# Hybrid decoder layer on one core: sample cross-attention on unsplit cache tiles, two couples fewer begun ahead, and a reordered feed-forward

## The chip, the core and the metric

The kernel runs on one core of a Trainium2 chip. The core has five engines, each with its own in-order instruction stream: TensorE (PE: matrix products into PSUM), VectorE (DVE), ScalarE (ACT), GpSimd (POOL) and SyncE (SP). Nearly all transfers between the chip's memory (HBM) and the core's SBUF are issued from SP, one after another, and carried out by 16 DMA engines. The metric is the device time of one launch in microseconds (us), the median of several runs.

## The reference, cut to what matters

One decoder layer, in fp32, for a prompt of 1024 tokens and eight sample sequences of 8 tokens each, width 1024. The branches ahead of the cross-attention are not touched by the change.

```
x <- LN1(alpha*x + branches(x))
qm = (x @ w_mq)                                  # 4 heads x 256
s  = einsum('nqhe,nkhe->nhqk', qm, mem_k) / 16   # 256 memory tokens
pr = softmax(s)
att = einsum('nhqk,nkhe->nqhe', pr, mem_v) @ w_mo
x <- LN2(alpha*x + att)
ff = square(relu(x @ w_up)) @ w_down             # 1024 -> 4096 -> 1024
x <- LN3(alpha*x + ff)
```

For the prompt, mem_k and mem_v are computed once. For the eight sample sequences they come from a cache with keys and values of each sequence's own: 8 x 256 x 1024 numbers each, 16.8 MB in all.

## The kernel before

Most products are made in the form float32r, in which a value is split into a high half (`whi`, `ah`, a rounding copy made by ACT) and a low half (`wlo`, `al`, the rest, a subtraction on DVE). One product of two split operands is three matmuls: high by high, high by low, low by high. A plain fp32 product of unsplit operands is also possible; the profile counts it as two matmul records (two passes).

**Cross-attention of the samples** (`sample_x`). This generator runs beside the prompt's cross-attention: each `yield` hands over to the prompt's scores (`sc`, line 129). The cache comes in 32 tiles of 128x1024 numbers (512 KB). `split_w` loads a tile into `wraw`, ACT casts it to `whi` (line 100) and DVE makes `wlo` (line 106). Then come 8 matmuls for each tile with the sample's query `qz` (scores, `sps`, line 1553) or probabilities `pz` (outputs, `ops`, line 1578) as the stationary operand of 64 columns: high and low halves side by side, 32 columns each. After the outputs, `spread` turns them with products with a selection matrix `sel` (`otr`, line 1566).

**Feed-forward, up** (`feed`). The 4096 hidden columns are made in 16 couples p of two tiles of `w_up` rows (`fetch(p)`, 1 MB). For each couple a fast scheme (Strassen's, in Winograd's form) makes a 2x2 block product in 7 products instead of 8. The operands are sums of weight blocks (`sw`: two sums on POOL in `first_sums`, two on DVE in `prep`) and sums of blocks of the turned activations (`hat`, by names: "11", "21", "t1" to "t4", "22"), all split in halves (`split`: ACT line 1686, DVE line 1687; `xht`, `xlt` are the activations' halves). Each product is 24 matmuls of 272 columns, 12 for each of two column blocks c. Two of the seven ("11" and "21") need only activations that are ready early. `begin(p)` makes these two ahead for the couples p < `EARLY_PAIRS`, while the last parts of the activations are still being normed; the results of couples from 2 on are put into HBM (`vd`) from a buffer `vs` and fetched again by `recall`. The main loop then runs over p. In it `store(p-1)` issues the eight stores of the couple before, `fetch(p+2)` the loads of the couple after next, `sums_in` and `sums_out` move the sums of `w_down`.

All these transfers go through `dma`, which keeps them in the written order on SP. So a load stands behind each store that is written ahead of it, and a store waits until its sums (`sh` on POOL, lines 1925 to 1928) are made.

**Feed-forward, down** (`down`). Again 7 products, each over 16 couples: 112 steps (i, p), in the order of products 1, 2, 6, 7, 5, 3, 4. A step is 12 matmuls of 512 columns (`dn`, line 1989), for products 1, 2, 7 and 3 also two for the samples (line 1994). Before step n, `bring(n + LOADS)` issues loads and `cut(n + SPLITS)` splits the operands `dop` of the step that comes two steps later. The last product keeps its last `TAIL` couples back and does them token tile by token tile at the end, so that the last norms (`finish`) can start one tile after another.

A scheduler with instruction costs decides how the streams that the generators offer are interleaved; within an engine the order then is fixed.

Of the kernel before, what the change touches and what calls it, by code (L numbers as in the profile page):

```python
# [8 lines left out]
F32 = mybir.dt.float32  # L9
# [32 lines left out]
LOADS, SPLITS, TAIL, OX = 4, 2, 6, 12  # L42

EARLY_PAIRS = 6
# [5 lines left out]
class Kern:  # L50
# [1457 lines left out]
    def sample_x(self, x1, out):  # L1508

        nc, I, pm = self.nc, self.I, self.pm
        sel = pm.tile([64, 32], F32, name="sel")
        nc.sync.dma_start(sel, I["sel"])
        z = pm.tile([128, 512], F32, name="zs")
        qs = pm.tile([128, 8, 64], F32, name="qs")
        row = lambda name: pm.tile([128, 512], F32, name=name, tag="row", bufs=2)

        def own(src, name):

            t = pm.tile([128, 4, 4, 64], F32R, name=name, tag="own", bufs=2)
            nc.vector.memset(t.rearrange("p a s x -> p (a s x)").bitcast(F32), 0.0)
            t4 = t.rearrange("p (a b) s x -> p a b s x", b=2)
            for s4 in range(4):
                v, c = src(s4), 8 * s4
                nc.scalar.copy(t4[:, :, :, s4, c:c + 8], v)
                nc.vector.tensor_sub(t4[:, :, :, s4, 32 + c:40 + c], v, t4[:, :, :, s4, c:c + 8].bitcast(F32))
# [16 lines left out]
        parts = [(s2, hp) for s2 in range(2) for hp in range(2)]  # L1544
        for s2, hp in parts:
            qz = own(lambda s4: qs[:, 4 * hp:4 * hp + 4, 32 * s2 + 8 * s4:32 * s2 + 8 * s4 + 8].rearrange("p (a b) q -> p a b q", b=2), "qz")
            ps = self.wk_ps("sps", "acc")
            for s4 in range(4):
                w = self.split_w(I["cmk"][4 * s2 + s4, hp])
                for h in range(2):  # L1550
                    for ct in range(2):
                        for i in range(2):
                            nc.tensor.matmul(ps[0:64, h * 256:h * 256 + 256], qz[:, 2 * h + ct, s4, :], w[i][:, (2 * h + ct) * 256:(2 * h + ct) * 256 + 256],
                                             start=s4 == h == ct == i == 0, stop=s4 == 3 and h == ct == i == 1)
                yield
            r, lo = slice(64 * s2 + 32 * hp, 64 * s2 + 32 * hp + 32), row("slo")
            nc.scalar.copy(lo[r], ps[32:64])
            nc.vector.tensor_add(z[r], lo[r], ps[0:32])
        pT = pm.tile([128, 4, 128], F32, name="pTs")
        nc.scalar.copy(pT, self.keys_first(self.softmax(z, "ps")))  # L1560
        pT = pT.rearrange("p (h k) (s a t) -> p k h s a t", k=2, s=2, a=2)
        def spread(s2, hp, o):

            tr = self.wk_ps("otr")[:, 0:128].rearrange("p (k t) -> p k t", t=32)
            for k in range(4):
                nc.tensor.matmul(tr[:, k, :], o[0:64, k * 128:k * 128 + 128], sel, start=True, stop=True)
            nc.scalar.copy(out[:, 4 * hp:4 * hp + 4, 32 * s2:32 * s2 + 32], tr)

        last = None
        for s2, hp in parts:  # L1570
            pz = own(lambda s4: pT[:, :, :, s2, hp, 8 * s4:8 * s4 + 8], "pz")
            ps = self.wk_ps("ops", "acc")
            for s4 in range(4):
                w = self.split_w(I["cmv"][4 * s2 + s4, hp])
                for kb in range(2):
                    for h in range(2):
                        for i in range(2):
                            nc.tensor.matmul(ps[0:64, h * 256:h * 256 + 256], pz[:, 2 * kb + h, s4, :], w[i][:, (2 * kb + h) * 256:(2 * kb + h) * 256 + 256],
                                             start=s4 == kb == h == i == 0, stop=s4 == 3 and kb == h == i == 1)
                if s4 == 1 and last:  # L1580
                    spread(*last)
                yield
            o = row("so")
            nc.scalar.copy(o[0:64], ps[0:64])
            last = s2, hp, o
        yield
        spread(*last)
# [76 lines left out]
    def feed(self, hat, y, s_xb, s_y, w3, w4, wb):  # L1664
# [103 lines left out]
        hat.rest("t4")  # L1768
        s_y.close()
# [29 lines left out]
        def operands():  # L1799
            for p in range(16):  # L1800
# [5 lines left out]
        todo, ops = operands(), []  # L1806
# [40 lines left out]
        steps = [(i, p) for i in (1, 2, 6, 7, 5, 3, 4) for p in range(16)]  # L1847
# [18 lines left out]
        first_sums(0)  # L1866
        for p in range(16):
# [38 lines left out]
            if p < 14:  # L1906
                fetch(p + 2)
            else:
                for n in range(2):
                    bring(2 * (p - 14) + n)  # L1910
# [40 lines left out]
        self.down(ring4, steps, bring, cut, ready, slots, late, dma)  # L1951

    def down(self, ring4, steps, bring, cut, ops, slots, late, dma):
# [9 lines left out]
        v, u2, u3 = ([yp.tile([128, 512], F32, name=f"{x}{j}") for j in range(4)] for x in ("v", "u2", "u3"))  # L1963
# [20 lines left out]
        def tokens(n, j, first, last):  # L1984
            hs, w = ops[n]
            c = slice(j * 128, j * 128 + 128)
            parts = [(0, 0), (1, 0), (0, 1)]
            for k, (a, b) in enumerate(parts):
                nc.tensor.matmul(ps[j], hs[:, a, c], w[:, b], start=first and k == 0, stop=last and k == 2, skip_group_check=n >= 16 and steps[n][0] in (2, 7, 3))  # L1989
# [7 lines left out]
        def evict(i, j):  # L1997
# [3 lines left out]
            if i == 1:  # L2001
                nc.scalar.copy(v[j], ps[j])
            elif i == 2:
                keep(a[:, lo], ps[j])
            elif i == 6:
                nc.vector.tensor_add(u2[j], v[j], ps[j])
                keep(a[:, hi], u2[j])
            elif i == 7:
                nc.vector.tensor_add(u3[j], v[j], ps[j])
                for c in HALVES:  # L2010
                    keep(b[:, c], u3[j])
            elif i == 5:
                add(b[:, hi])
            elif i == 3:
                add(a[:, hi])
            else:
                nc.vector.tensor_sub(b[:, lo], b[:, lo], ps[j])

        def evict_sample(i):
# [3 lines left out]
            if i == 2:  # L2023
                nc.vector.scalar_tensor_tensor(lo, lo, ALPHA, sp[0:64], op0=ALU.mult, op1=ALU.add)
                nc.gpsimd.tensor_add(lo, lo, ex)
            elif i == 7:
                nc.vector.scalar_tensor_tensor(hi, hi, ALPHA, sp[0:64], op0=ALU.mult, op1=ALU.subtract)
                nc.gpsimd.tensor_sub(hi, hi, ex)
            elif i == 3:
                nc.vector.tensor_add(hi, hi, sp[0:64])  # L2030
                nc.gpsimd.tensor_add(hi, hi, ex)
# [11 lines left out]
        nsteps = len(steps)  # L2043
        for n, (i, p) in enumerate(steps):
            if n >= SPLITS:
                bring(n + LOADS)
            cut(n + SPLITS)
# [9 lines left out]
            if p == 0 and i in (1, 6, 5, 4):  # L2057
# [3 lines left out]
            starts = i in (1, 6, 5, 4)  # L2061
# [24 lines left out]
            if i == 3 and p < 4:  # L2086
# [100 lines left out]
def _consts():  # L2187
# [31 lines left out]
    return {"sel": np.tile(np.eye(32, dtype=f), (2, 1)), "cmask": cm, "amask": am, "tmask": tm, "smask": np.tile(sm, (128, 1)), "teye": te.reshape(128, 8, 32), "ident": np.eye(128, dtype=f)}  # L2219
# [98 lines left out]
```

## Time and profile before

| what | value |
|---|---|
| median of 3 runs | 2275.94 us (2272.01 to 2283.53) |
| the profiled execution's own time | 2281.47 us |
| its span, first to last instruction | 2279.7 us |
| mean granted TensorE clock | 0.977 of full speed |
| PE busy | 2175.1 us, 95% of the span, 13702 instructions |
| DVE, ACT, POOL busy | 1374.5 (60%), 978.7 (43%), 425.7 (19%) us |
| HBM traffic | 157 GB/s mean over the span |

In the profiled execution the branches end near 1297 us; then come the cross-attention (to 1443), the projection with `w_mo` and the second norm (to 1546), the first part of the feed-forward with its `begin` calls (to 1602), the up loop (to 1924), the down product (to 2268), and the last norm and stores. PE is the busiest engine in every one of these stages but the last, so the rows are read for two things: how long PE takes for its work, and where it waits.

### The profile page before, as it was taken

How to read it: one execution, taken by the hardware profiler on the slowest of the kernel's cores; microseconds unless marked ns; L12 is line 12 of the kernel's file. 1: busy time of each engine (PE TensorE's matmuls, PEld its weight loads, DVE VectorE, ACT ScalarE, POOL GpSimd, SP SyncE). 2: the span in 40 equal slices, each digit the busy share in tenths (PEclk: the TensorE clock that was granted, in tenths of full speed). 3: DMA queues.
4: the chain of work that ended last, by engine and by line, in shares of the span. 5: the costliest groups of instructions: out<-in, count | busy, mean ns of one | idle time of the engine just before them, and what ended most of it. 6: DMA issues, size and time to landing. Idle time of an engine off the chain costs nothing.

```text
span 2279.7 us, 36377 instructions
## 1 busy us (share of the span) xinstructions
PE 2175.1 (95%) x13702; PEld 1949.2 (86%) x13702; DVE 1374.5 (60%) x2748; ACT 978.7 (43%) x1888; POOL 425.7 (19%) x484
## 2 busy tenths in 40 slices
PE   8998999999999999999999999998789999999997
PEld 8987777898989888998998888778789999788886
DVE  3356767755665764343333877586667776655558
ACT  4333433145555655444231566335334444543432
POOL 0111111012311200123220500000445444100100
PEclk9998989999999999999999999999899999999999
DMA  5322333135444435555324355624487767975534
GB/s 191 103 75 61 99 90 98 38 129 186 152 132 130 130 114 171 162 173 162 102 64 149 120 190 167 221 102 141 162 292 261 248 238 239 325 240 182 178 118 171
DMA packets 186071, 359.41 MB, mean 158 GB/s; under 512 B 36312, under 2 KB 92776, under 8 KB 185896
## 3 DMA queue, kind: packets, MB, share of 16 engines
q1 hardware_dynamic: 175448, 321.52, 43.2%
q0 software_dynamic: 10448, 35.57, 4.6%
q8 instruction: 108, 1.77, 0.3%
q14 instruction: 67, 0.55, 0.1%
HBM read 252.18 MB, written 104.84 MB: 157 GB/s over the span
## 4 chain that ended last, share of the span: by engine, by line
PE 71%; DVE 10%; DMA 9%; issue 4%; ACT 3%; POOL 2%; SPq 1%; DVEq 0%; ACTq 0%; POOLq 0%
PE mm L117 21%; PE m L117 12%; PE dn L1989 11%; PE mm L129 8%; PE sc L129 3%; PE pp L117 3%; PE ds L1994 1%; DVE tpr L1013 1%; DVE wlo L106 1%; DMA vp<-in_vpages,pt 1%; ACT whi L100 1%; DMA Li<-Ld 1%; PE wtp L502 1%; DVE Ti L1014 1%; PE gr L965 1%
## 5 line engine op out<-in xcount | busy, mean ns | idle before, releaser
L117 PE MATMUL mm<-ah,whi 128*128 128x384 f32 (+1 forms) x1176 | 395.7, 336 | 8.4 <-ACT ah L277 4.9
L117 PE MATMUL mm<-al,whi 128*128 128x384 f32 (+1 forms) x1176 | 392.5, 334 | 0.6 <-DVE al L278 0.6
L117 PE MATMUL mm<-ah,wlo 128*128 128x384 f32 (+1 forms) x1176 | 391.7, 333 | 0.6 <-DVE wlo L106 0.6
L1989 PE MATMUL dn<-dop 128*128 128x512 f32 x1344 | 318.8, 391 | 3.7 <-ACT dop L1686 3.5
L1989 PEld LDWEIGHTS dn<-dop 128*128 128x128 f32 x1344 | 251.7, 188 | 60.6 <-ACT dop L1686 5.2
L106 DVE TENSOR_TENSOR wlo<-wraw,whi 128x1024 fp32r<-128x1024 f32 (+2 forms) x177 | 196.1, 1117 | 174.1 <-ACT whi L100 172.6
L100 ACT CAST whi<-wraw 128x1024 fp32r<-128x1024 f32 (+1 forms) x162 | 165.8, 1032 | 258.0 <-PE mm L117 101.6
L117 PEld LDWEIGHTS mm<-ah,whi 128*128 128x128 f32 x1176 | 224.4, 191 | 18.0 <-ACT ah L277 5.5
L117 PEld LDWEIGHTS mm<-al,whi 128*128 128x128 f32 x1176 | 224.1, 191 | 7.0 <-issue 3.5
L117 PEld LDWEIGHTS mm<-ah,wlo 128*128 128x128 f32 x1176 | 224.1, 191 | 4.3 <-issue 1.9
L1687 DVE TENSOR_TENSOR dop<-wraw,dop 128x512 fp32r<-128x512 f32 x224 | 151.3, 712 | 118.2 <-ACT dop L1686 117.6
L117 PE MATMUL m<-xht,wo 128*128 128x272 f32 x1024 | 202.7, 293 | 16.8 <-ACT wo L1686 10.5
L1686 ACT CAST dop<-wraw 128x512 fp32r<-128x512 f32 x224 | 131.2, 619 | 167.8 <-PE dn L1989 117.3
L117 PEld LDWEIGHTS m<-xht,wo 128*128 128x128 f32 x1024 | 165.8, 192 | 17.7 <-ACT wo L1686 10.7
L129 PE MATMUL mm<-wlo,ah 128*128 128x512 f32 (+1 forms) x488 | 170.1, 351 | 2.7 <-DVE wlo L106 2.7
L129 PE MATMUL mm<-whi,ah 128*128 128x512 f32 (+1 forms) x488 | 170.5, 351 | 0.8 <-ACT stA L300 0.5
L117 PE MATMUL m<-xh,wo 128*128 128x272 f32 x768 | 153.6, 293 | 6.1 <-DVE r L1901 6.1
L129 PE MATMUL mm<-whi,al 128*128 128x512 f32 (+1 forms) x448 | 156.5, 349 | 0.0
L117 PE MATMUL m<-xlt,wo 128*128 128x272 f32 x512 | 149.5, 292 | 0.0
L117 PEld LDWEIGHTS m<-xh,wo 128*128 128x128 f32 x768 | 124.7, 192 | 6.7 <-ACT wo L1686 2.6
L117 PE MATMUL m<-xl,wo 128*128 128x272 f32 x384 | 111.9, 292 | 0.0
L129 PEld LDWEIGHTS mm<-wlo,ah 128*128 128x128 f32 x488 | 93.9, 193 | 16.7 <-DVE wlo L106 3.6
(510 smaller groups left out, 4313.1 us busy)
## 6 DMA issues: line engine op xcount, KB each, us to landing
wraw<-hs SPq DMA_DIRECT2D x112, 256.0 KB
wraw<-in_w_up SPq DMA_DIRECT2D x38, 512.0 KB
wraw<-in_w_gate SPq DMA_DIRECT2D x32, 512.0 KB
dw<-in_w_down SPq DMA_DIRECT2D x32, 512.0 KB
hs<-sh SPq DMA_DIRECT2D x64, 256.0 KB
wt<-dw SPq DMA_DIRECT2D x32, 512.0 KB
wraw<-wt SPq DMA_DIRECT2D x64, 256.0 KB
wraw<-in_w_down SPq DMA_DIRECT2D x48, 256.0 KB
```

The source lines that it names most:

```text
L100: nc.scalar.copy(hi[:, c], raw[:, c])
L106: nc.vector.tensor_sub(lo[:, c], raw[:, c], hi[:, c].bitcast(F32))
L117: nc.tensor.matmul(ps[:, :n], a, b, start=first and i == 0, stop=last and i == len(steps) - 1, skip_group_check=not first)
L129: nc.tensor.matmul(ps[:, :n], a, b, start=i == 0, stop=i == len(steps) - 1)
L502: self.nc.tensor.transpose(ps[:b.shape[-1], j * 128:j * 128 + 128], b, self.ident)
L965: nc.tensor.matmul(g[hh][:nb, j, :nb], p[HR[hh], pr, cs], q[HR[hh], pr, cs], start=True, stop=True)
L1013: nc.vector.tensor_mul(tv, Ti[:, 0:h, 0:t + 1], Li[:, 0:t + 1, t:t + 1].rearrange("p s o -> p o s").to_broadcast([128, h, t + 1]))
L1014: nc.vector.tensor_reduce(Ti[:, 0:h, t:t + 1], tv, axis=AX.X, op=ALU.add)
L1686: nc.scalar.copy(o[:, 0], src)
L1687: nc.vector.tensor_sub(o[:, 1], src, o[:, 0].bitcast(F32))
L1989: nc.tensor.matmul(ps[j], hs[:, a, c], w[:, b], start=first and k == 0, stop=last and k == 2, skip_group_check=n >= 16 and steps[n][0] in ...
L1994: nc.tensor.matmul(sp, rows[p][:, smp[i]].rearrange("p a n -> p (a n)"), ops[n][1][:, b], start=i != 2 and p == 0 and b == 0, stop=p == 15 ...
```

## The change

1. `sample_x`: a cache tile stays as it is (`kvraw`, fp32). Two tiles make a pair; for a pair there are 8 fp32 matmuls with a stationary operand of 32 columns, each writing one of four groups of 32 output partitions (`r = 64 * h + 32 * s`). The casts and subtractions of the cache tiles go, and so does `sel`; the outputs are turned by 4 transposes. A tile's buffer is free again when PE has read it (before: when DVE had).
2. `EARLY_PAIRS` is 4 in place of 6. `fetch(0)` stands ahead of `begin(2)`, and the operands of couple 0 are made from it in place, on DVE, and split before the last activations (`rest("t4")`).
3. In the up loop, for p < 4, `fetch(p + 2)` stands ahead of `store(p - 1)` and `recall(p + 1)`.
4. Down: products in the order 1, 2, 6, 5, 3, 7, 4, the seventh in new accumulators; buffers `v` and `u` in pools of two, which `widen` hands to the operands once they are free; 15 slots `ox` in place of 12; the splits' lead grows from 2 steps to 6 between steps 64 and 80 (`FAR`); `TAIL` is 8 in place of 6; the norms of the first token tiles move from product 4 into product 7.

```diff
-LOADS, SPLITS, TAIL, OX = 4, 2, 6, 12
+LOADS, SPLITS, FAR, TAIL, OX = 4, 2, 4, 8, 15
-EARLY_PAIRS = 6
+EARLY_PAIRS = 4
...
+        def raw(src):
+            self.wi += 1
+            t = self.raws[self.wi % len(self.raws)].tile([128, 1024], F32, name="kvraw", tag="raw")
+            nc.sync.dma_start(t, src)
+            return t
+
+        def products(ps, o, name, hp, col, first, last):
+            for j in range(4):
+                w = []
+                for a in range(2):
+                    w.append(raw(I[name][2 * j + a, hp]))
+                    if a:
+                        for i in range(2):
+                            for h in range(2):
+                                c, st = col(h, i)
+                                for s in range(2):
+                                    r = 64 * h + 32 * s
+                                    nc.tensor.matmul(ps[r:r + 32, o:o + 256], st[:, s, j, :], w[s][:, 256 * c:256 * c + 256],
+                                                     start=first and j == i == 0, stop=last and j == 3 and i == 1)
+                    yield
...
-        for s2, hp in parts:
-            qz = own(lambda s4: qs[:, 4 * hp:4 * hp + 4, 32 * s2 + 8 * s4:32 * s2 + 8 * s4 + 8].rearrange("p (a b) q -> p a b q", b=2), "qz")
-            ps = self.wk_ps("sps", "acc")
-            for s4 in range(4):
-                w = self.split_w(I["cmk"][4 * s2 + s4, hp])
+        for hp in range(2):
+            qz = own(lambda j: qs[:, 4 * hp:4 * hp + 4, 16 * j:16 * j + 16].rearrange("p k (s q) -> p k s q", q=8), "qz")
+            yield from products(ps, 256 * hp, "cmk", hp, lambda h, ct: (2 * h + ct, qz[:, 2 * h + ct]), hp == 0, hp == 1)
...
         hat.second(y, 6, self.gp)
+        fetch(0)
         begin(2)
         hat.second(y, 7, self.gp)
         begin(3)
-        begin(4)
-        begin(5)
-        fetch(0)
+        a11, a12, a21, a22 = blocks(0)
+        x0 = hat.pool.tile([128, 512], F32, name="x0", tag="ex8", bufs=1)
+        nc.vector.tensor_sub(x0, a11, a21)
+        nc.vector.tensor_add(a21, a21, a22)
+        nc.vector.tensor_sub(a11, a21, a11)
+        nc.vector.tensor_sub(a12, a12, a11)
+        ops = [split(a11)]
+        hat.rest("t3")
+        ops.append(split(x0))
+        hat.rest("t1")
+        ops.append(split(a21))
         fetch(1)
-        hat.rest("t3")
-        hat.rest("t1")
         s_t4.close()
         hat.room(s_up.enter_context(self.pool("xh4", side="right")), ("t4",))
         hat.rest("t4")
+        ops.append(split(a22))
...
-        steps = [(i, p) for i in (1, 2, 6, 7, 5, 3, 4) for p in range(16)]
+        steps = [(i, p) for i in (1, 2, 6, 5, 3, 7, 4) for p in range(16)]
...
-            if p:
+            if p >= EARLY_PAIRS:
                 store(p - 1)
-            if 1 <= p < EARLY_PAIRS - 1:
-                recall(p + 1)
             if 3 <= p < 15:
                 first_sums(p + 1)
             w5 = nxt()
+            if p < EARLY_PAIRS:
+                fetch(p + 2)
+                if p:
+                    store(p - 1)
+                if 1 <= p < EARLY_PAIRS - 1:
+                    recall(p + 1)
...
-            if p < 14:
+            if EARLY_PAIRS <= p < 14:
                 fetch(p + 2)
...
+        def widen(*rooms):
+            k = st["slot"] % len(slots)
+            slots[:], st["slot"] = [*rooms, *slots[k:], *slots[:k]], 0
...
-            if n >= SPLITS:
-                bring(n + LOADS)
-            cut(n + SPLITS)
+            while done <= n + SPLITS + min(FAR, max(0, (n - 64) // 4)):
+                if done >= 2 * SPLITS:
+                    bring(done + LOADS - SPLITS)
+                cut(done)
+                done += 1
+            if i == 5 and p == 0:
+                widen(*[(pv, "vv")] * 2)
+            if i == 4 and p == 0:
+                widen(*[(pu, "uu")] * 2)
...
-            if i == 4 and p in (1, 3, 5, 7, 9):
-                finish({1: 0, 3: 1, 5: 2, 7: 3, 9: 8}[p])
+            if i == 7 and p in (1, 4, 7, 10):
+                finish(p // 3)
+            if i == 4 and p == 4:
+                finish(8)
```

How the change moves instructions shows at three places. The first is PE in the cross-attention, where the samples' scores `sps` lie among the prompt's scores `sc`. Before:

```order
L1553 MATMUL sps<-wlo,qz 64x256
L1553 MATMUL sps<-whi,qz 64x256
L1553 MATMUL sps<-wlo,qz 64x256
L129 MATMUL sc<-whi,ah_12520 128x512
L1553 MATMUL sps<-whi,qz 64x256
L129 MATMUL sc<-whi,al_12523 128x512
L129 MATMUL sc<-wlo,ah_12520 128x512
L129 MATMUL sc<-whi,ah_12520 128x512
```

The same place in the changed kernel:

```order
L130 MATMUL sc<-whi,al_12522 128x512
...
L130 MATMUL sc<-whi,al_12523 128x512
L1544 MATMUL sps<-kvraw,qz 32x256 x8
L130 MATMUL sc<-wlo,ah_12520 128x512
...
L1544 MATMUL sps<-kvraw,qz 32x256 x16
L1506 MATMUL ptr<-ident,p 128x128 x4
L130 MATMUL sc<-whi,ah_12520 128x512
```

The 64-column products, high and low half in turn, became bursts of 8 or 16 fp32 products of 32 columns; over the stage there are 12 such bursts for the 16 pairs of tiles, mostly 24 score products apart.

The second place is DVE at the end of the activations' last part, where the up loop begins (`xlt` is the low half of "t4", `wo` a weight operand, `sw` a sum of weights, `u` the first result of the loop). Before:

```order
L1687 TENSOR_TENSOR wo<-wraw,wo 128x512
L2127 TENSOR_TENSOR xlt_15628<-xtb,xht_15627 128x4x128 x4
L2127 TENSOR_TENSOR xlt_15628<-xt_15118,xht_15627 128x8x16
L1792 TENSOR_TENSOR sw<-wraw 128x512
L1794 TENSOR_TENSOR sw<-wraw,sw 128x512
L1687 TENSOR_TENSOR wo<-sw,wo 128x512 x3
L1687 TENSOR_TENSOR wo<-wraw,wo 128x512
L1792 TENSOR_TENSOR sw<-wraw 128x512
L1880 TENSOR_TENSOR u_15647<-vr,m_15663 128x272
```

After:

```order
L1692 TENSOR_TENSOR wo<-x_15123,wo 128x512
L1772 TENSOR_TENSOR wraw<-wraw 128x512
L2163 TENSOR_TENSOR xlt_14765<-xta,xht_14764 128x4x128
L1692 TENSOR_TENSOR wo<-wraw,wo 128x512 x3
L2163 TENSOR_TENSOR xlt_15166<-xtb,xht_15165 128x4x128 x4
L2163 TENSOR_TENSOR xlt_15166<-xt_14772,xht_15165 128x8x16
L1692 TENSOR_TENSOR wo<-wraw,wo 128x512
L1894 TENSOR_TENSOR u_15184<-vr,m_15187 128x272
```

The splits of couple 0's operands moved from behind the four `xlt` of "t4" to ahead of them; the first `u` stands behind these `xlt` in both.

The third place is SP's queue in the first turns of the up loop (`wraw<-in_w_up` is `fetch`, `hs` and `hsm` the stores, `v<-vd` and `r<-vd` a `recall`). Before:

```order
L1749 DMA vd<-vs 128x1088 x2
L1695 DMA wraw<-in_w_up 128x1024 x2
L1695 DMA dw<-in_w_down 128x1024 x2
L1695 DMA hs_106<-vr 256x1x256
...
L1695 DMA hsm<-sm 128x128
L1695 DMA v<-vd 128x544
L1695 DMA r_15918<-vd 128x544
L1695 DMA wraw<-in_w_up 128x1024 x2
L1695 DMA wt<-dw 128x1024 x2
```

After:

```order
L1700 DMA wraw<-in_w_up 128x1024 x2
L1700 DMA dw<-in_w_down 128x1024 x2
L1700 DMA wraw<-in_w_up 128x1024 x2
L1700 DMA hs_106<-vr 256x1x256
...
L1700 DMA hsm<-sm 128x128
L1700 DMA v<-vd 128x544
L1700 DMA r_15446<-vd 128x544
L1700 DMA wt<-dw 128x1024 x2
```

The load of couple 3 moved from behind the eight stores of couple 0 and the recall to ahead of them; the recall is still behind the stores.

## Rows read from the trace of the kernel before

**Rows 1.** Windows by stage: each engine's busy time, granted clock, DMA share.

```profile
core 0: us, PE busy (x) PEld busy (x) DVE busy (x) ACT busy (x) POOL busy (x), PEclk, DMA share, GB/s
1297.00:1443.00 146.00, 144.88 (x809) 119.55 (x808) 114.35 (x215) 90.89 (x193) 7.47 (x6) 1.00 0.56 182
...
1593.00:1607.00 14.00, 5.27 (x23) 5.27 (x24) 9.24 (x13) 3.79 (x8) 6.24 (x5) 0.51 0.22 77
...
1641.00:1648.00 7.00, 4.31 (x19) 4.34 (x20) 5.90 (x7) 0.00 (x0) 6.87 (x6) 0.51 0.76 236
1648.00:1710.00 62.00, 55.92 (x437) 55.30 (x436) 39.73 (x72) 24.11 (x40) 29.08 (x31) 0.99 0.86 286
```

**Rows 2.** PE's timeline in the cross-attention: start, us, line, operation, count.

```profile
1407.09 1.08 PE L1566 MATMUL otr<-sel,so 64*128 64x32 f32 x8
1408.10 0.66 PE L1505 MATMUL ptr<-ident,p 128*128 128x128 f32 x4
...
1408.83 0.28 PE L1578 MATMUL ops<-wlo,pz 128*64 128x256 f32 x1
...
1409.76 0.60 PE L1505 MATMUL ptr<-ident,p 128*128 128x128 f32 x4
```

**Rows 3.** PE's timeline, fp32 products of 128, 32 and 64 stationary columns.

```profile
230.04 1.12 PE L917 MATMUL hs<-xr,cmask 128*128 128x512 f32 x2
231.01 1.02 PE L917 MATMUL hs<-Y,cmask 128*128 128x512 f32 x2
...
552.53 0.63 PE L518 MATMUL zp<-kp,qb 128*32 128x128 f32 x8
553.09 0.42 PE L117 MATMUL mm<-ah,whi 128*128 128x320 f32 x1
...
639.34 1.07 PE L558 MATMUL ysp<-vp,wP 128*32 128x128 f32 x16
640.33 1.09 PE L446 MATMUL yps<-wT,v 128*64 128x128 f32 x16
```

**Rows 4.** PE's waits in the up loop: total us, times, longest.

```profile
PE m L117 <- ACT wo L1686: 10.5, 1, 10.5
PE m L117 <- DVE u L1880: 6.2, 2, 5.7
PE m L117 <- DVE r L1901: 6.1, 3, 2.4
```

**Rows 5.** Timeline of all engines ahead of the loop; in brackets idle before, releaser.

```profile
1595.23 2.50 DVE L2127 TENSOR_TENSOR xlt<-xtb,xht 128x512 fp32r<-128x512 f32 x4 [14.44 <-DMA vd<-vs]
...
1598.07 1.58 POOL L1779 TENSOR_TENSOR sw<-wraw 128x512 f32<-128x512 f32 x1 [45.52 <-DVE xlt L2127]
...
1601.06 1.66 ACT L1686 CAST wo<-sw 128x512 fp32r<-128x512 f32 x3 [6.45 <-POOL sw L1780]
...
1601.73 0.59 PE L117 MATMUL m<-xht,wo 128*128 128x272 f32 x1 [10.51 <-ACT wo L1686]
```

**Rows 6.** Timelines of DVE and ACT in the up loop.

```profile
1639.77 1.76 DVE L1792 TENSOR_TENSOR sw<-wraw 128x512 f32<-128x512 f32 x1 [4.34 <-DMA wraw<-in_w_up]
...
1686.80 1.66 ACT L1686 CAST wo<-sw 128x512 fp32r<-128x512 f32 x3 [8.44 <-POOL sw L1780]
```

**Rows 7.** PE's timeline at the end of the down product.

```profile
2251.03 5.48 PE L1989 MATMUL dn<-dop 128*128 128x512 f32 x18 [0.92 <-ACT dop L1686]
2256.97 11.34 PE L1989 MATMUL dn<-dop 128*128 128x512 f32 x48 [0.46 <-ACT dop L1686]
```

**Rows 8.** DVE's timeline at the very end.

```profile
2269.41 0.68 DVE L2017 TENSOR_TENSOR y<-y,dn 128x512 f32<-128x512 f32 x1
...
2270.13 0.69 DVE L2038 BATCH_NORM_STATS2 bn<-y 128x6 f32<-128x512 f32 x1
...
2273.58 1.41 DVE L1454 SCALAR_TENSOR_TENSOR y<-y,mv,lng 128x512 f32<-128x512 f32 x2
...
2275.09 1.41 DVE L1457 SCALAR_TENSOR_TENSOR y<-y,rs,lnb 128x512 f32<-128x512 f32 x2
```

More of the change, by code (lines that the diff above doesn't have):

```diff
@@ L1559, in sample_x @@
[L1559 to L1567, printed above, removed]
+        ps = self.wk_ps("sps", "acc")
@@ new lines, in sample_x, with spread @@
+        for hp in range(2):
+            qz = own(lambda j: qs[:, 4 * hp:4 * hp + 4, 16 * j:16 * j + 16].rearrange("p k (s q) -> p k s q", q=8), "qz")
+            yield from products(ps, 256 * hp, "cmk", hp, lambda h, ct: (2 * h + ct, qz[:, 2 * h + ct]), hp == 0, hp == 1)
+        pT = pm.tile([128, 4, 128], F32, name="pTs")
+        nc.scalar.copy(pT, self.keys_first(self.softmax(ps, "ps")))
+        pT = pT.rearrange("p k (g j q) -> p k g j q", j=4, q=8)
+        def spread(hp, o):
+            tr = self.wk_ps("otr")
+            for k in range(2):
+                nc.tensor.transpose(tr[:, 128 * k:128 * k + 128], o[:, 128 * k:128 * k + 128], self.ident)
+            for k in range(2):
+                for h in range(2):
+                    nc.scalar.copy(out[:, 4 * hp + 2 * h + k, :].rearrange("p (j s q) -> p s j q", s=2, q=8),
+                                   tr[:, 128 * k + 64 * h:128 * k + 64 * h + 64].rearrange("p (s j q) -> p s j q", s=2, q=8))
@@ L1569, in sample_x @@
         last = None
-        for s2, hp in parts:
-            pz = own(lambda s4: pT[:, :, :, s2, hp, 8 * s4:8 * s4 + 8], "pz")
+        for hp in range(2):
+            pz = own(lambda j: pT[:, 2 * hp:2 * hp + 2, :, j, :].rearrange("p k (h s) q -> p (k h) s q", s=2), "pz")
             ps = self.wk_ps("ops", "acc")
[L1573 to L1580, printed above, removed]
+            for i, _ in enumerate(products(ps, 0, "cmv", hp, lambda h, kb: (2 * kb + h, pz[:, 2 * kb + h]), True, True)):
+                if i == 2 and last:
@@ L1583, in sample_x @@
             o = row("so")
-            nc.scalar.copy(o[0:64], ps[0:64])
-            last = s2, hp, o
+            nc.scalar.copy(o[:, 0:256], ps[:, 0:256])
+            last = hp, o
         yield
@@ L1799, in operands @@
         def operands():
-            for p in range(16):
+            yield split(blocks(0)[1])
+            for p in range(1, 16):
                 yield from prep(p)
@@ L1804, in operands @@
                     yield split(raw[n][:, o:o + 512], "dop")
-        todo, ops = operands(), []
+        todo = operands()
         def nxt():
@@ L1905, in feed @@
             w4_ = nxt()
-            if p < 14:
+            if EARLY_PAIRS <= p < 14:
                 fetch(p + 2)
-            else:
+            elif p >= 14:
                 for n in range(2):
@@ L1962, in down @@
         y = [yp.tile([128, 1024], F32, name=f"y{t}") for t in range(9)]
-        v, u2, u3 = ([yp.tile([128, 512], F32, name=f"{x}{j}") for j in range(4)] for x in ("v", "u2", "u3"))
+        pv, pu = (ctx.enter_context(self.pool(x, 2)) for x in ("vv", "uu"))
+        v, u = ([a[:, j] for a in [pool.tile([128, 2, 512], F32, name=x, tag=x) for _ in range(2)] for j in range(2)] for pool, x in ((pv, "vv"), (pu, "uu")))
         stats = [yp.tile([128, 2, 6], F32, name=f"bn{j}") for j in range(4)]
@@ L1988, in tokens @@
             for k, (a, b) in enumerate(parts):
-                nc.tensor.matmul(ps[j], hs[:, a, c], w[:, b], start=first and k == 0, stop=last and k == 2, skip_group_check=n >= 16 and steps[n][0] in (2, 7, 3))
+                nc.tensor.matmul(ps[j], hs[:, a, c], w[:, b], start=first and k == 0, stop=last and k == 2, skip_group_check=n >= 16 and steps[n][0] in (2, 3))
         def sample(n):
@@ L2056, in down @@
                 dma(gb[p // 4 - 1], I["ln"][3 + p // 4])
-            if p == 0 and i in (1, 6, 5, 4):
+            if p == 0 and i in fresh:
                 ps = {j: self.mm_ps("dn") for j in range(4)}
@@ L2060, in down @@
                 sp = pss.tile([128, 512], F32, name="ds", tag="ds")
-            starts = i in (1, 6, 5, 4)
+            starts = i in fresh
             if i == 4 and p >= 16 - TAIL:
```

56 lines of the change are left out of this document (20 added, 36 removed).

## The prediction, made before the changed kernel ran

> **What bounds the kernel now.** I read the windows by stage first, because shares over the whole span say little. In the cross-attention PE is busy for 144.88 of 146 us at full clock [rows 1], so only less work on PE can shorten that stage. The up loop is different: PE's list of waits there names 10.5 us for a ScalarE split, 6.2 and 6.1 us for VectorE results [rows 4]. The reader should look at the clock beside these waits. In the window with the longest of them PE made 23 products at a clock of 0.51, and in the one with the 5.7 us wait 19, also at 0.51 [rows 1]: TensorE worked at 1.2 GHz, the lower of its two levels, after having stood still. The timelines then tell which engine or transfer each wait goes back to. At the end of the kernel PE has finished and VectorE is still norming [rows 8].
>
> The sum is made against the profiled execution's own 2281.47 us (span 2279.7); it stands 5.5 us over the median of 2275.94. I take what the profile loses off the median.
>
> **The cross-attention.** Removed are 256 products of 256 columns, 0.116 us each (eight of them between 1408.83 and 1409.76 [rows 2]), so 29.6 us, and four turns with `sel` of 1.01 us (1407.09 to 1408.10), 4.0 us. The four new transposes cost as much as the four `ptr` between 1408.10 and 1408.51, about 0.4 us. The splits that go (32 casts, 32 subtractions) lie beside PE and give nothing of themselves.
>
> New are 128 fp32 products, 256 records of 256 columns. A full-width fp32 record of 512 columns takes 0.485 us (two between 230.04 and 231.01 [rows 3]), so one of 256 columns 0.24 us. Without overlap the new work would take 256 x 0.24 = 61 us. But narrow products do overlap: eight records of 128 columns took 0.56 us and sixteen 0.99 us [rows 3]. The difference gives 0.43 us for eight, 0.054 us each, less than half of 0.485/4 = 0.121; the rest, 0.13 us, is the cost of the change of form at a burst. These are two column groups side by side. Four groups never occur in this trace, so the cost has two bounds:
> - four side by side: a pair of tiles has 16 records, 4 rounds of 0.215 us, 0.86 us; 16 pairs 13.8 us, 12 bursts at 0.13 us 1.6 us: 15.4 us. Gain 33.6 - 15.8 = 17.8 us.
> - two side by side: 8 rounds, 1.72 us; 27.5 + 1.6 + 0.4 = 29.5 us. Gain 4.1 us.
>
> I take the first, since two groups overlap without loss in the rows and the new order offers the four groups one right after the other.
>
> The Trainium skill ("TensorE: Matmul & The Clock Gate", Part 2) speaks against it: of the four streams that feed the column groups it calls that of the last quadrant not supported, and its table of packings (Part 3, "Measured speedup vs the span model") has three column tiles at 2.38 times, none with four columns alone. By 2.38 the new work would be 61 / 2.38 = 26 us and the gain of this part 6 us; no run here shows three or four groups yet.
>
> The buffers of the cache tiles are now freed by PE. Between bursts lie 24 score products of 512 columns, 24 x 0.236 = 5.7 us (11.34 us for 48 [rows 7]). A pair of tiles is 1.05 MB; at the 286 GB/s that the up loop sustained [rows 1] it lands in 3.7 us, and the ring holds two pairs. Over the stage 12 x 5.7 + 13.8 = 82 us are there for 16 pairs, 205 GB/s, above the stage's 182 [rows 1] but below 286. I put 2.8 us of waits (bounds 0 and 10: 16.8 MB at 182 GB/s would need 92 us). **Term: -15.**
>
> **The start of the up loop.** The 10.5 us are a chain [rows 5]: VectorE's `xlt` waits for the store of `vs`, whose buffer it takes over, starts at 1595.23; POOL's first sum waits for VectorE until 1598.07 and its second ends at 1601.06 when ScalarE splits; PE starts at 1601.73. After, couple 0's operands are split ahead of these `xlt`, and POOL is out of the chain. Two `begin` calls are gone from here (their 96 products come back in the loop, at no change of work). 96 x 0.128 us (437 products in 55.92 us [rows 1]) is 12.3 us. So PE is through with the `begin` calls at 1601.73 - 10.51 - 12.3 = 1578.9, and the store that `xlt` waits for lands near 1583 in place of 1595.23. Product 6 of couple 0 (24 products, 3.1 us) needs no "t4" and can fill this time. What is late next is product 7: it adds into the accumulators that VectorE's `u` must have read, and `u` stands in VectorE's order behind the `xlt` (2.50 us), a small one and a split (0.3 and 0.7): near 1587. So PE's waits ahead of products 6 and 7 are 1587 - 1578.9 - 3.1 = 5 us together, and 5.5 go. At half clock 23 products cost 23 x 0.128 = 2.9 us too much; of this I count 1.5, since the waits left over may cost some clock too. **Term: -7** (bounds -3 and -13).
>
> **The turns of the loop.** The 5.7 us wait goes back to a load: VectorE's sum for couple 3 starts at 1639.77 after waiting 4.34 us for `w_up` [rows 6], and this load stands behind `store(0)`, which waits for POOL. After, `fetch(3)` is ahead of it. The three waits of together 6.1 us [rows 4] follow from ScalarE's splits, which come after POOL's sums (8.44 us idle ahead of 1686.80 [rows 6]), which wait for their late blocks in turn; loads that come ahead of stores let the sums start early. Also, the window of early couples moves 0.86 of what the DMA engines can [rows 1]; with four early couples there are two `vd` stores and recalls less. So 12.3 - 0.4 us of waits and 2.2 us of clock (half of 4.31 us busy at 0.51) can go, 14 in all. `recall` still stands behind the stores, two times, for which I leave 2. **Term: -12** (bounds -3 and -14).
>
> **Down and the end.** The order of products changes no count. The waits for `dop` at 2251.03 and 2256.97 (0.92 and 0.46 us [rows 7]) go with the longer lead of the splits: -1.4. After the last accumulator VectorE needs from 2269.41 to 2276.50, 7.1 us [rows 8], as the tile before is not normed yet. A tile held back by 8 couples gives VectorE 24 x 0.236 = 5.7 us for a tile in place of 18 x 0.236 = 4.2. One tile alone needs 0.68 + 0.69 + 1.41 + 1.41 and 0.3 of small ones, 4.5 us, so the backlog goes: -2.6. The norms moved into product 7 are VectorE's work beside PE's steps of 12 x 0.236 = 2.8 us; uncovered, each would hold up the splits by its 4.5 us, which a lead of 6 steps takes. **Term: -4.**
>
> **Sum:** -15 - 7 - 12 - 4 = -38, from 2281.47 to about 2243 in the profile, and from 2275.94 to **2238** in the median.
>
> **The rivals.**
> - *Only two column groups overlap*, or the fourth is made behind the other three: two rounds for four products either way. Gain of the first term 4 in place of 15 (no waits for loads, since PE is slower): 2238 + 11 = 2249. For it: no row has more than two. Against it: these two overlap fully. Chance 0.15. The Trainium skill's page and sections named above are on this rival's side.
> - *The waits of the feed-forward move and don't vanish*: product 7 waits as above and at half clock after it, and `recall`, behind eight stores, delays each early couple. The feed-forward's two terms come to -9 in place of -19: 2248. For it: DMA at 0.86 of its share there. Chance 0.15.
> - *No overlap at all*, because four groups with four different moving operands are made one after the other: 61 + 1.6 + 0.4 - 33.6 = +29.4, the others -23: 2282, no change that can be told. Against it stand the rows at 552.53 and 639.34. Chance 0.03.
> - *Slower*: PE frees the tiles now, so each burst could wait for its pair. A burst and the scores behind it last 0.9 + 5.7 = 6.6 us. If a pair takes 9.6 us in place of 3.7, each of 12 bursts waits 3 us, and as the clock was 0.51 through 7 us after a wait of 5.7 [rows 1], each wait costs up to 2.2 us more: 12 x 5.2 = +62, less 17.8 and 23: 2276 + 21 = 2297. It decides where the 12 waits eat these 41 us, 3.4 each with the clock's 2.2, so from some 8 us for a pair (131 GB/s). Against it: 182 GB/s were moved here even before. Chance 0.04.
>
> **How the numbers follow.** The forecast has 0.63; its own range is 2227 (no waits at the loads, the feed-forward's terms at their best, -27) to 2245. The first two rivals end at 2249 and 2248, and both together at 2259. Lowest 2222, as the runs before lie up to 7 us from their median; highest 2259. Left out are the last two rivals, both rivals in a worse form, and a better case than all bounds: under 0.2. A measurement here can tell about 0.5%, 11 us, from no change. Faster by more: forecast and two rivals, 0.93, of which I give 0.02 to the middle for their tails: 0.91. Same: 0.05. Slower: 0.04.
>
> **What would show it.** Right: the stage of the cross-attention lasts about 131 us with PE near full, and 16 new records take about 0.86 us; if they take 1.7 us the first rival holds, at 3.8 us the third. The 10.5 us wait becomes 5 us in all ahead of products 6 and 7, the last part released by `u`; no wait of over 2 us stands in the turns p = 1 to 3, and VectorE's wait for `w_up` is gone. No wait for `dop` in the last 30 us; the last matmul is followed by some 8 us in place of 11. Wrong: PE waiting for `kvraw` ahead of bursts, or a clock of 0.51 anywhere in the cross-attention.

## The result and the profile after

The changed kernel takes 2234.29 us (median of 4 runs, 2232.75 to 2238.48), the kernel before beside it 2273.98 (4 runs): 39.7 us less, a ratio of 0.983 (95% interval 0.981 to 0.985). The forecast was 2238, with 38 us to be gained.

The two profiled executions differ by more, 2279.7 to 2231.0 us of span, 48.7. The stages show why. A stage is measured here from the first prompt score to the first product of the feed-forward, from there to the first down product, to the last down product, and to the end, always from start to start:

| stage, us | before | after | change | forecast |
|---|---|---|---|---|
| branches, not touched | 1297.5 | 1290.6 | -6.9 | 0 |
| cross-attention and projection | 249.8 | 232.1 | -17.7 | -15 |
| feed-forward up to the first down product | 376.8 | 356.4 | -20.4 | -19 |
| down product | 343.8 | 342.5 | -1.3 | -1.4 |
| behind the last product | 11.8 | 9.4 | -2.4 | -2.6 |

The first row is not the change's: in the profiled executions of the twelve other kernels of this study the same branches took 1285.8 to 1297.9 us. The changed stages sum to -41.8.

In the changed kernel's cross-attention the bursts stand in PE's timeline as follows.

```profile
1344.21 2.04 PE L1544 MATMUL sps<-kvraw,qz 128*32 128x256 f32 x32
1346.18 0.66 PE L1506 MATMUL ptr<-ident,p 128*128 128x128 f32 x4
...
1352.33 1.07 PE L1544 MATMUL sps<-kvraw,qz 128*32 128x256 f32 x16
1353.33 0.66 PE L1506 MATMUL ptr<-ident,p 128*128 128x128 f32 x4
```

From 1344.21 to the next form at 1346.18 are 1.97 us for 32 records, and 1.00 for the 16 from 1352.33: 0.062 us a record. The forecast's four rounds and one change of form make 0.86 + 0.13 = 0.99 for 16. Nothing stands in brackets: PE never waited for a cache tile.

The windows of the changed kernel, cut at its own stages (same columns as [rows 1]):

```profile
1290.00:1420.00 130.00, 128.31 (x782) 94.72 (x780) 67.32 (x138) 52.39 (x137) 7.47 (x6) 1.00 0.57 194
...
1522.00:1553.00 31.00, 28.10 (x206) 27.86 (x205) 28.16 (x53) 19.20 (x44) 1.07 (x2) 0.89 0.40 142
1553.00:1562.00 9.00, 6.94 (x43) 6.72 (x43) 8.87 (x14) 6.02 (x14) 2.35 (x2) 0.81 0.31 111
1562.00:1607.00 45.00, 45.00 (x359) 45.00 (x358) 36.17 (x59) 18.71 (x31) 24.43 (x22) 1.00 0.71 246
1607.00:1618.00 11.00, 7.75 (x49) 7.56 (x49) 7.80 (x15) 3.83 (x7) 6.86 (x8) 0.84 0.79 259
1618.00:1879.00 261.00, 261.00 (x2072) 261.00 (x2071) 189.24 (x286) 122.35 (x222) 122.81 (x121) 1.00 0.71 245
```

Three windows have a lower clock: 0.89 around the `begin` calls, and 0.81 and 0.84 in two short ones. Between these two and behind them PE is busy for every microsecond. PE's list of waits from the loop's start names the two causes:

```profile
PE m L118 <- DVE u L1894: 3.2, 1, 3.2
PE m L118 <- ACT wo L1691: 2.1, 1, 2.1
```

Against [rows 4], 22.8 us of waits became 5.3. The wait for ScalarE stands at the loop's start:

```profile
1555.06 0.69 DVE L1771 TENSOR_TENSOR wraw<-wraw 128x512 f32<-128x512 f32 x1
...
1555.97 0.61 ACT L1691 CAST wo<-wraw 128x512 fp32r<-128x512 f32 x1
...
1556.48 0.66 ACT L1733 ACTIVATE vs<-vs 128x544 f32<-128x544 f32 x1
...
1557.04 1.13 ACT L1691 CAST wo<-wraw 128x512 fp32r<-128x512 f32 x2
...
1557.68 3.00 DVE L1692 TENSOR_TENSOR wo<-wraw,wo 128x512 fp32r<-128x512 f32 x3
...
1557.70 0.60 PE L118 MATMUL m<-xht,wo 128*128 128x272 f32 x1 [2.06 <-ACT wo L1691]
...
1560.60 2.48 DVE L2163 TENSOR_TENSOR xlt<-xtb,xht 128x512 fp32r<-128x512 f32 x4
...
1564.91 0.77 DVE L1894 TENSOR_TENSOR u<-vr,m 128x272 f32<-128x272 f32 x2
```

The splits `wo` of couple 0 now come ahead of the `xlt`, as the order of instructions said. PE has nothing left at 1555.64 and waits 2.06 us for ScalarE's split of product 6's operand. VectorE has made this operand by 1555.75 (line 1771), but in ScalarE's order another split and a square come first. PE then runs on while VectorE works through `xlt` and reaches `u` at 1564.91 only. The wait for `u` stands ahead of product 7 of couple 3:

```profile
1603.97 0.32 SPq L1700 DMA_DIRECT2D v<-vd  x1
1604.00 0.62 ACT L1691 CAST wo<-wraw 128x512 fp32r<-128x512 f32 x1 [4.00 <-DMA hs<-vr]
...
1606.70 0.69 DVE L1692 TENSOR_TENSOR wo<-wraw,wo 128x512 fp32r<-128x512 f32 x1 [3.73 <-ACT wo L1691]
...
1610.54 0.78 DVE L1894 TENSOR_TENSOR u<-v,m 128x272 f32<-128x272 f32 x2
...
1611.12 0.37 PE L118 MATMUL m<-xht,wo 128*128 128x272 f32 x1 [3.25 <-DVE u L1894]
```

ScalarE's split waited 4.00 us, not for a weight, but for a store of `vr` (`hs<-vr`) to land; VectorE waited behind it for 3.73 us and came late to `u`; PE waited 3.25.

The end, VectorE's timeline, answers to [rows 8]:

```profile
2216.59 0.69 DVE L2044 TENSOR_TENSOR y<-y,dn 128x512 f32<-128x512 f32 x1 [0.81 <-PE dn L2016]
...
2222.03 0.69 DVE L2044 TENSOR_TENSOR y<-y,dn 128x512 f32<-128x512 f32 x1 [0.81 <-PE dn L2016]
...
2225.25 1.41 DVE L1458 SCALAR_TENSOR_TENSOR y<-y,rs,lnb 128x512 f32<-128x512 f32 x2
```

An eviction every 5.44 us, each tile normed before the next: 4.6 us from the last eviction to 2226.66, where it was 7.1.

### The profile page after: what moved, and what is told of

Same layout as the page of the kernel before. It is cut to its first block, busy times and chain, and to the rows that moved or that the text cites. A ratio compares the mean times of both kernels' runs of the same rounds, so it can differ in the third digit from the quotient of the medians.

```text
span 2231.0 us, 36111 instructions
## 1 busy us (share of the span) xinstructions
PE 2146.9 (96%) x13674; PEld 1918.4 (86%) x13674; DVE 1342.9 (60%) x2678; ACT 945.1 (42%) x1838; POOL 424.2 (19%) x482
## 4 chain that ended last, share of the span: by engine, by line
PE 74%; DVE 9%; DMA 9%; ACT 3%; issue 3%; POOL 1%; SPq 1%; DVEq 0%; ACTq 0%; POOLq 0%
PE mm L118 22%; PE m L118 14%; PE dn L2016 13%; PE mm L130 8%; PE sc L130 3%; PE pp L118 3%; DVE tpr L1014 1%; PE ds L2021 1%; PE gr L966 1%; DVE wlo L107 1%; DVE Ti L1015 1%; DMA vp<-in_vpages,pt 1%; DMA Li<-Ld 1%; PE wtp L503 1%; ACT whi L101 1%
## 5 line engine op out<-in xcount | busy, mean ns | idle before, releaser
L107 DVE TENSOR_TENSOR wlo<-wraw,whi 128x1024 fp32r<-128x1024 f32 (+2 forms) x145 | 158.9, 1104 | 173.0 <-ACT whi L101 170.1
L101 ACT CAST whi<-wraw 128x1024 fp32r<-128x1024 f32 (+1 forms) x130 | 132.9, 1027 | 228.3 <-PE mm L118 100.5
```

What stands on the lines that cost most here:

```text
L101: nc.scalar.copy(hi[:, c], raw[:, c])
L107: nc.vector.tensor_sub(lo[:, c], raw[:, c], hi[:, c].bitcast(F32))
```

## The experiments

Each kernel ran beside the kernel before, whose median was 2274 to 2276 us every time. Runs of one kernel spread by 3.6 to 13.7 us, those of the kernel before by up to 19.4, so the stage table further down serves them all. A stage spreads too: the up stage is the same code in the changed kernel and in four of the kernels below (`group_order`, `two_groups`, `split_cache`, `old_down`), and their profiled executions took 350.5 to 359.4 us for it.

**Column groups in another order** (`group_order`).

```diff
-  for i in range(2):
+  for s in range(2):
       for h in range(2):
-          for s in range(2):
+          for i in range(2):
```

> The changed kernel (2234 us) with the same eight fp32 products for each pair of cache tiles, written so that the column groups come as 0,0,2,2,1,1,3,3 in place of 0,1,2,3,0,1,2,3. Theory (the gain of the unsplit cache comes from four column groups working side by side, and a product starts only once those ahead of it have started and its own group is free): five rounds in place of two, 5 x 0.43 = 2.15 us for a pair of tiles in place of 0.97, 16 pairs: +19, about 2253 us. Rival (the products are taken to free groups whatever their order, or the gain comes from the splits that are gone): no change, 2232 to 2237 us.

2232.58 us (2231.79 to 2235.35), no change: the theory's rule on order fell. In its timeline a burst looks like this:

```profile
1339.79 2.04 PE L1544 MATMUL sps<-kvraw,qz 128*32 128x256 f32 x32
...
1347.90 1.09 PE L1544 MATMUL sps<-kvraw,qz 128*32 128x256 f32 x16
```

It takes the same time as before within 0.02 us for 16 records. In both runs nearly all of the single records start in rounds of four, as a rule within 20 ns of each other in the changed kernel and 40 ns here, and a round starts about 0.22 us after the one before. So order doesn't matter; whether four groups do was still to be tested.

**Two groups only** (`two_groups`).

```diff
-  r = 64 * h + 32 * s
+  r = 64 * hp + 32 * s      # both heads h add into the same 64 partitions
```

> The changed kernel, in which the products of both heads of a pair of cache tiles write the same 64 output partitions, so that only two column groups are used at a time; number, size and order of the products stay, and the samples' scores and outputs are not the reference's. Theory (the gain of the unsplit cache comes from four groups working side by side): 16 records of a pair take 1.72 us in place of 0.97, the stage up to the feed-forward is longer by 16 x 0.8 = 12 to 14 us, 2246 to 2249 us. Rival (two groups already use up what the operands' paths to TensorE carry): no change, 2232 to 2237 us, as in the run with the groups in another order.

```profile
1346.32 3.65 PE L1544 MATMUL sps<-kvraw,qz 128*32 128x256 f32 x32
...
1356.04 1.92 PE L1544 MATMUL sps<-kvraw,qz 128*32 128x256 f32 x16
```

Number and size of the products are the same; the accumulators are set to zero first, and the flags that begin and end a sum follow the new rows. A record takes 0.114 us (3.65 us for 32), where the changed kernel's row has 0.064 (2.04 us for 32), and the records start in rounds of two, again about 0.22 us apart. An accumulator is now written by every second product, but this is not the cause: the run before wrote each twice in a row and lost 0.02 us a burst. The stage is 244.7 us in place of 232.1, +12.6; the total 2242.61 (2240.48 to 2246.71), +8, as in this run's profile the feed-forward was 3.2 us shorter and what follows it 2.1. Four groups side by side are shown, and they are worth 12.6 us of the 17.7; with two, 5.1 would be left, where the prediction's second bound had 4.1.

**The split cache put back** (`split_cache`).

```diff
-  (sample_x on kvraw, fp32)
+  (sample_x of before: whi, wlo, products of 64 columns)
```

> The changed kernel with the cross-attention of the samples as it was before (tiles split in halves, products of 64 columns). Theory: the stage of the cross-attention gave 17.7 us of the profile's gain, so about 2252 us, and 256 products at 0.116 us are seen again. Rival (part of this came from the profiled execution of before, which was a long one, or the part of the gain is paid for in the next stage): 2238 to 2246 us.

2249.21 us (2245.22 to 2249.86). Its stage lasts 249.9 us, 17.8 more than in the changed kernel, the theory's size. The median is +15. The two profiled executions differ by 17.1: 17.8 of this stage and 7.3 of the untouched branches, less 2.1 behind the feed-forward and 5.9 in it (350.5 us, at a granted clock of 1.00 in place of 0.98; its first 48 products took 10.8 us in place of 13.2, and the wait ahead of couple 3's product 7 was 2.0 in place of 3.2).

**The unsplit cache alone, in the kernel before** (`unsplit_alone`).

> The kernel before with the unsplit cache tiles alone. Theory (the parts of the change do not lean on each other): the stage up to the feed-forward is 17.7 us shorter, 2256 to 2258 us, and the waits of 10.5 and 5.7 us in the feed-forward stay as they were. Rival (part of the gain is taken back, because the next stages start with other loads or a lower clock): 2260 to 2268 us.

2261.59 us (median of 7, 2255.02 to 2268.72), ratio 0.994 (0.991 to 0.996), between theory and rival; the interval, 8.6 to 19.6 us of gain, holds the theory's 17.7. The stages settle it: cross-attention 232.2 (-17.6), feed-forward 376.9 as before, and its waits nearly so (24.5 us in place of 22.8):

```profile
PE m L117 <- ACT wo L1690: 10.5, 1, 10.5
PE m L117 <- DVE u L1884: 8.5, 2, 6.7
PE m L117 <- DVE r L1905: 5.5, 3, 2.7
```

Nothing is taken back by the feed-forward; the down product and end of this execution were 1.9 us longer than before's.

**Loads behind stores again** (`loads_behind`).

```diff
-  if p < EARLY_PAIRS:
-      fetch(p + 2)
-      if p: store(p - 1)
-      if 1 <= p < EARLY_PAIRS - 1: recall(p + 1)
+  if p: store(p - 1)                              # ahead of w5
+  if 1 <= p < EARLY_PAIRS - 1: recall(p + 1)
+  if p < 14: fetch(p + 2)                         # behind w4
```

> The changed kernel with the early turns of the up loop issuing stores, recall and loads in the order of before (load of the couple after next behind the stores), everything else as changed. Theory (this order alone made the wait of 5.7 us in the turns and most of the 6.1 us of smaller ones): waits of together 8 to 11 us come back with about 2 us of clock, 2242 to 2247 us. Rival (two couples fewer begun ahead took the load off the transfers, and the order matters little): 2233 to 2237 us.

```profile
PE m L118 <- DVE u L1894: 8.9, 3, 7.0
PE m L118 <- DVE r L1916: 2.4, 1, 2.4
```

2242.89 us (2237.16 to 2246.42), feed-forward 364.5, +8.1, and above all of the 350.5 to 359.4 us with the new order. VectorE's sum for a new couple waits for `w_up` again, 5.67 us at 1597.71:

```profile
1597.71 1.76 DVE L1806 TENSOR_TENSOR sw<-wraw 128x512 f32<-128x512 f32 x1 [5.67 <-DMA wraw<-in_w_up]
```

The rival falls: with two couples fewer the order still counts.

**Six couples begun ahead** (`six_early`, and `six_early_2` with the operands in order).

```diff
-EARLY_PAIRS = 4
+EARLY_PAIRS = 6
...
         begin(3)
+        begin(4)
+        begin(5)
```

> The changed kernel with six couples begun ahead in place of four, the two further ones behind the third; couple 0's operands are split ahead of the last activations as in the changed kernel, and the early turns are now six. Theory (the start of the loop gained because couple 0's operands come ahead of the last activations, not because there is less begun ahead; two stores and recalls more make the early turns wait): the wait ahead of the loop stays under 3 us, the turns wait 2 to 6 us more, 2236 to 2241 us. Rival (the two couples fewer are what took the 10.5 us wait away): it comes back in part, over 5 us ahead of the loop. Third: the two couples give VectorE time to be ready, and the total falls to 2231 us or below.

> The run with six couples begun ahead, with the operands now in their right order (in the run before, the test for couples begun ahead looked too early, so that some operands went to another product). Theory and rivals as there: under 3 us of waiting ahead of the loop and 2233 to 2241 us if it is the early operands that count; over 5 us ahead of the loop if it is the two couples fewer.

2233.06 us (2226.75 to 2237.5), and with the operands in order 2230.3 (2225.86 to 2238.75); feed-forward 355.9, against 356.4 with four. Its waits:

```profile
PE m L118 <- DVE u L1896: 2.9, 2, 1.9
...
PE m L118 <- DVE xlt L2165: 2.0, 1, 2.0
```

No wait stands ahead of the loop's first product; the 2.0 us for `xlt` come two products later. So the early operands took the 10.5 us away. The second half of the theory missed: the turns wait 2.9 us for `u`, not longer than with four. The two couples fewer give nothing that can be measured here.

**Sums on GpSimd** (`pool_sums`). The four sums for couple 0 go from `nc.vector` to `nc.gpsimd`.

> The changed kernel with the four sums for couple 0's operands on GpSimd in place of VectorE. Theory (the 2.1 us wait ahead of the loop is VectorE being busy for 28 of the 31 us before it): the wait goes, with about 1.5 us of clock, 2230 to 2233 us. Rival (GpSimd needs about twice as long for each sum, 1.6 us, four in a chain, and is late itself): the wait is 3 to 6 us, 2235 to 2239 us.

2235.72 us (2232.82 to 2243.24), which is no change that the total could tell. The wait for ScalarE is gone, but 1.8 us for `xlt`, 1.1 for `vs` and 0.8 for `wo` came, 3.7 together, the size that the rival had.

**The recall first** (`recall_first`).

```diff
   fetch(p + 2)
+  if 1 <= p < EARLY_PAIRS - 1:
+      begun[p + 1] = tile("v", 1)
+      dma(begun[p + 1], self.vd[p + 1, :, 0])     # r11 stays behind the stores
   if p: store(p - 1)
```

> The changed kernel with one more edit: of what is fetched again for the early couples 2 and 3, the part that product 6 and 7 need is issued ahead of the eight stores of the couple before, the other part behind them as it was. Theory (the one wait left in the turns, 3.2 to 5.1 us ahead of product 7 of couple 3, is that recall standing behind the stores): the wait goes, with 1 to 2 us of clock, 2229 to 2231 us. Rival (the wait comes from the transfers' share, not their order): it stays or moves to a store or load, 2233 to 2236 us.

2229.99 us (2222.17 to 2234.37), in the theory's range, but by luck. The wait was 2.6 us, within the 2.0 to 5.1 that it had in the five executions without this edit; ScalarE waited for `hs<-vr` again, 2.0 us; and the granted clock was 1.00 in the whole up stage. The theory named the wrong cause.

**The larger ring of slots one couple later**, alone (`wide_later`) and with the recall first (`wide_recall`).

```diff
-  if p == 3:
+  if p == 4:
       st["wide"], st["slot"] = True, 0
```

> The changed kernel with one edit: the ring of operand slots grows from four to six from couple 4 on, in place of couple 3. Theory (formed after the recall run: ScalarE's split for couple 3 waits 4.0 us for the store that still reads the first results of couple 1, which lie in the two slots that the larger ring takes over, and VectorE and TensorE wait behind it): the 3.2 us wait goes and with it 1 to 2 us of clock, 2229 to 2231 us. Rival (four slots are too few for couple 3, or the recall behind the stores is the wait): a wait of 2 us or more stays ahead of product 7 of couple 3 or comes ahead of another product, 2232 to 2237 us.

> The changed kernel with both edits for couple 3: the recall of what products 6 and 7 need ahead of the stores, and the ring of six slots from couple 4 on. Theory (the slots made the wait): as with the slots alone, 2229 to 2231 us, no wait over 1 us left in the turns, feed-forward up to the first down product about 350 us. Rival (both causes are needed): 2 to 4 us less than with the slots alone.

Alone 2227.23 us (2222.0 to 2233.7), and the wait is 1.3, below all five without this edit. ScalarE's splits between 1598 and 1609 us now wait for PE alone and for no store:

```profile
1604.92 0.62 ACT L1691 CAST wo<-wraw 128x512 fp32r<-128x512 f32 x1 [1.12 <-PE m L118]
```

With the recall first as well 2226.22 us (2223.91 to 2228.18), feed-forward 350.1, and one wait is left in the loop, at its start:

```profile
PE m L118 <- ACT wo L1691: 2.1, 1, 2.1
```

So the slots made the store part of the wait. How the rest divides between slots and recall is not shown, with one execution of each and 2.0 to 5.1 us where neither was changed. This version, ratio 0.979 (0.976 to 0.981), is the fastest of the study; its runs and those of the changed kernel (2232.75 to 2238.48) don't overlap. Its up stage by itself would not show it: `split_cache`, with the changed kernel's loop, had 350.5.

**The down product of before** (`old_down`), with its order, lead, slots and six couples kept back.

> The changed kernel with the down product as before: products in the order 1, 2, 6, 7, 5, 3, 4, lead of the splits 2 steps, six couples kept back, 12 slots. Theory: the waits for operands near the end (1.3 us) and the backlog of the last norms (2.4 us) come back, 2238 us. Rival (these parts are within noise, or the new order costs what its ending gains): 2232 to 2235 us, and the last matmul is again followed by 11 us or more.

2242.62 us (median of 5, 2231.41 to 2242.97). The total can't tell 4 us with such a spread. The stages can: down 344.9 (+2.4) and 11.9 behind the last product (+2.5), 4.9 together, somewhat more than the theory's 3.7. The end is as the theory had it. Of the 2.4 us, 0.7 are waits, only 0.5 of them near the end, where the kernel before had 1.4; PE's busy time is 1.7 us longer (339.8 against 338.1), for which no run shows the cause.

| stage, us | to first score | cross-attention | up | down | end |
|---|---|---|---|---|---|
| group_order | 1286.2 | 232.7 | 359.4 | 342.4 | 9.4 |
| two_groups | 1291.9 | 244.7 | 353.2 | 341.5 | 8.3 |
| split_cache | 1297.9 | 249.9 | 350.5 | 341.6 | 8.2 |
| unsplit_alone | 1292.0 | 232.2 | 376.9 | 345.7 | 11.8 |
| loads_behind | 1295.6 | 230.9 | 364.5 | 342.5 | 8.3 |
| six_early_2 | 1294.3 | 231.2 | 355.9 | 341.4 | 8.3 |
| pool_sums | 1291.8 | 232.3 | 357.3 | 342.1 | 8.3 |
| recall_first | 1287.2 | 232.2 | 350.8 | 341.9 | 8.3 |
| wide_later | 1291.1 | 233.0 | 351.7 | 342.8 | 8.3 |
| wide_recall | 1292.5 | 231.7 | 350.1 | 341.2 | 8.3 |
| old_down | 1285.8 | 231.9 | 355.1 | 344.9 | 11.9 |

## Why the prediction was right, step by step

- *Cross-attention, -15: -17.7.* Four groups do work side by side, as the first bound had it: the 12 bursts, each up to the next form, take 15.6 us, where the bound had 15.4, and the products that went took 30.4, where it had 29.6. Too small was the gain, by the 2.8 us put down for waits at the loads: there were none; pairs landed in time at the 194 GB/s of that window. The first rival is refuted by the run with two groups, the third by the same rows, and the slower case by the stage's full clock. (That case took its price from 7 us at a clock of 0.51; 2.7 of them were still the wait, and PE worked at this clock for 4.3.) The Trainium skill ("TensorE: Matmul & The Clock Gate", Part 2) has the last quadrant's stream as not supported. The traces here show no such limit: products with outputs in partitions 96 to 127 ran beside the others, with 0.064 us a record for four groups against 0.114 for two.
- *Start of the loop, -7: -8.4* (up to the 313th of the feed-forward's 2688 matmuls in the up stage, so after equal work; it starts 60.1 us after the first one before, and 51.7 after). The cause was right. The step that product 7 is late next failed: `u` was late, 10 us behind the last `begin` product where 8 were forecast, but the order on PE had put product 5 and part of 4 of couple 0 ahead of product 7, which begins with the loop's 59th matmul, at 1566.58. So nothing waited for `u`. The order of instructions showed this ahead of the run; it was read for VectorE only. The 2 us that were left are a wait that the prediction did not have: of product 6, for a split that stands behind another split and a square in ScalarE's order.
- *Turns, -12: -12.0* (316.7 to 304.6 us from that matmul on). With the step above this refutes the second rival, which had -9 for both. Most of it is the loads' place in SP's queue: the run that put it back took 314.8 us here, 10.1 more than the changed kernel, and 7 to 13 more than the four others with the same loop (301.9 to 307.7). The forecast that no wait of over 2 us is left was wrong: 3.2 us stood ahead of product 7 of couple 3. Here the prediction left out that ScalarE's split takes a slot whose old content a store has still to read, 4.0 us of waiting for ScalarE; what part the recall has in it, which the prediction named, is not shown. What it wrote of fewer couples taking load off the transfers found no support.
- *Down and end, -4: -3.7.* The backlog of norms is gone as worked out, 7.1 us behind the last eviction became 4.6. That the down product comes to -1.3 for the forecast's -1.4 is in part luck. The two waits near its end are gone, 1.4 us, but those in its first 30 us grew from 3.5 to 4.4, and PE's busy time fell by 0.8 us (338.9 to 338.1), which the prediction did not have and no run explains.

The sum of the steps, -38, and of the stages, -41.8, differ by little more than the waits put down for the loads.

## What to carry to other kernels

Products with few stationary columns cost little if their outputs lie in different groups of 32 partitions: unsplit fp32, four at a time, took 15.6 us here where split halves took 30.4. In a queue that all transfers share, what is needed next belongs ahead of what can wait; the loads' place was worth some 10 us. When a wait moves, look at the order on every engine, the one that would wait too, and at whose buffer the late instruction writes.

## What the hardware showed that was not expected

The order in which narrow products are issued made no difference (2232.6 against 2234.3 us, 1.09 against 1.07 us a burst), so a product for a free group is not held up by one ahead of it whose group is busy; held up, it would have made a pair's 0.97 us into 2.15, by the expectation's count. The Trainium skill ("TensorE: Matmul & The Clock Gate", Part 3, "The mechanism") has products start and end strictly in their order. These two runs speak against it for column groups: in `group_order` the first two products share a group, and still four records start within 40 ns.

The same wait did not cost the same clock each time. After the 2.06 us at the loop's start the granted clock was 0.76 in the changed kernel (1555 to 1562 us) and 1.00 at the same place in `recall_first` (1549 to 1556) and `split_cache` (1578 to 1586). Code that no kernel here changed took 1285.8 to 1297.9 us from one execution to the next, and the same up stage 350.5 to 359.4. So parts of a few us can't be told by the total, and in the up stage not by one profile's stage time either, but by the waits in it.
